# Running token tile 0 five jobs ahead in two blocks, with norm pieces transposed in that order and scaled by two engines

## The chip, the core and the metric

The kernel runs on one core of a Trainium2 chip. The core has a matmul engine (TensorE, PE in the profile), VectorE (DVE), ScalarE (ACT), GpSimd (POOL) and SyncE (SP), which run their own instruction queues in order, and DMA engines. The metric is the time of one execution in microseconds on the device.

## The reference

Two blocks follow each other on 256 tokens of width 2048, in float32. The first has two layers: a projection `x @ w_in`, two kinds of attention and a convolution, an output projection, and a layer norm. The second has an attention stage with a context, a gated merge of four branches, and a SwiGLU feed-forward network (FFN). What matters here are the places where a norm over the whole width stands between two matrix products:

```python
    y = jnp.concatenate([ya, yb, yc], axis=-1) @ w_out
    return layer_norm(ALPHA * x + y, ln_g, ln_b)      # then x @ w_in of the next layer
...
        x = x + g1 * merge_branches(h, branches, w_gate[i], w_branch, w_o[i])
        x = x + g2 * swiglu(modulate(rms_norm(x, norm2_w[i]), sh2, sc2),
                            w_ffn_gate[i], w_ffn_up[i], w_ffn_down[i])
```

A token's norm needs all 2048 columns of the product before it, and the product after it needs the normed row, transposed.

## The kernel before

**Products.** All large products run through `Kernel.run`. A block is one product of all 256 tokens (two token tiles t of 128) with 512 output columns. It is cut into jobs; a job brings 256 rows of the weights (512 KB). To keep float32 accuracy with fast matmuls, both factors are split into a high part (rounded, written by ScalarE) and a low part (what is left, written by VectorE), and each product is three matmuls: high x high, high x low weight, low x high weight. A unit is one 128-row half of a job with one tile, three matmuls; a step is four units, 12 matmuls, normally one job: halves kk = 0, 1, and within each the tiles 0 and 1. A block of 8 jobs has 96 matmuls.

**Steps.** Each step issues in this order: ScalarE's high parts of the weights that come up (`high`, L343; up to four jobs ahead, six buffers), one advance of each running background task (`step_tasks`), VectorE's low parts of the same weights (`low`, L351) with the load of a job four further on, perhaps a piece of another reduction on VectorE (`wmod_step`), and then its matmuls. The queues of the engines hold the instructions in just this order. A block may name `pre_t`, which makes the background task run on, at that place in the queues, until enough pieces are issued (`need`).

**Tail.** The last block ahead of a norm (of `w_out`, of `w_o`) has `tail` = 5: its last five jobs run with tile 0 first (10 units) and then with tile 1 (10 units), so that tile 0 is finished two and a half steps before tile 1. The sums of a finished tile are taken out of PSUM by `ev_out` or `ev_o` (VectorE, with statistics; a root on GpSimd), and at tile 0's end the norm's task is added.

**Pieces.** The task (`split_t`) works on eight pieces: column group g (512 columns) and tile t, in the order TILES = (0,0), (1,0), (0,1), (1,1), (2,0), (2,1), (3,0), (3,1). For each piece: a row-wise norm (`norm` L701 or `scaled` L792, on ScalarE; group 0 of the layer norm on VectorE), four 128 x 128 transposes on TensorE into one PSUM tile, four scalings by columns' scale and bias out of it on VectorE (tile `f`), the high part on ScalarE (L284) and the low part on VectorE. One round of the loop issues the low part of piece n-3, the scalings of piece n-1, norms up to two pieces ahead, the transposes of piece n and the high part of piece n-2. The task's first advance issues two norms; the second only yields.

**Boundaries.** The first block of layer 2 (columns 6656 on) and the FFN's first gate block have `pre_t`. READY = [3, 4, 6, 8] says how many pieces must be issued before a job of column group 0, 1, 2, 3 may run, so both tiles of group 0 before the first matmul. The task `lam` (two loads, a few VectorE instructions, an Exp) is started with the first block of a layer. The same `split_t` with scale and bias is used for the context (`context`) and for the norm between layer 2 and the second block (`layer_end` with l = 1, then `rms_t`); their blocks have no head.

Of the kernel before, what the change touches and what calls it, by code (L numbers as in the profile page):

```python
# [15 lines left out]
ALU = mybir.AluOpType  # L16
# [12 lines left out]
SPLIT = 1.15  # L29
LOOK = 4  # L30
ROWS = 13
TAIL, END = 5, 3

TILES = [(0, 0), (1, 0), (0, 1), (1, 1), (2, 0), (2, 1), (3, 0), (3, 1)]
READY = [3, 4, 6, 8]

WMOD_STEPS = {0: (22, 146), 1: (160, 274), 3: (290, 380), 4: (380, 470), 2: (470, 552), 5: (552, 612)}

# [74 lines left out]
class Block:  # L113


    def __init__(self, w, src, evac=None, pairs=None, pre=None, start=None, evac_t=None, pre_t=None, tail=0):
        self.w = w
        self.src = src
        self.evac = evac
        self.evac_t = evac_t  # L120
        self.pre_t = pre_t
        self.tail = tail
        self.pairs = list(range(w.shape[0])) if pairs is None else pairs
        self.pre = pre
        self.start = start
        self.ps = None


class Kernel:
# [99 lines left out]
        nc.gpsimd.tensor_tensor(r[:, 0:n], r[:, 0:n], self.half[:, 0:n], op=ALU.pow)  # L229
        return r  # L230

    def split_t(self, items, ahead=0):


        nc = self.nc
        n = 0
        xs = deque(it[0]() for it in items[:ahead])
        got = ahead
        yield n
        if ahead:  # L240
            yield n
        if items[0][3] is None:
            for src, hi, lo, _, _ in items:
                x = src()
                p = self.aux()
                for j in range(4):
                    nc.tensor.transpose(p[:, j * 128:(j + 1) * 128], x[:, j * 128:(j + 1) * 128], self.ident)
                yield n
                p3 = p.rearrange("p (j t) -> p j t", j=4)
                nc.scalar.activation(hi, p3, AF.Copy)  # L250
                yield n
                nc.vector.tensor_tensor(lo, p3, hi, op=ALU.subtract)
                n += 1
            yield n
            return
        ps, fs = {}, {}
        nt = nf = nh = nl = 0
        while nl < len(items):
            t, f, h = nt, nf, nh
            if nl < h:  # L260
                nc.vector.tensor_tensor(items[nl][2], fs.pop(nl), items[nl][1], op=ALU.subtract)
                nl += 1
            if nf < t:
                _, _, _, sc, bi = items[nf]
                p3 = ps.pop(nf).rearrange("p (j t) -> p j t", j=4)
                o = fs[nf] = self.h([128, 4, 128], name="f")
                for j in range(4):
                    nc.vector.tensor_scalar(o[:, j], p3[:, j], sc[:, j:j + 1], bi[:, j:j + 1],
                                            op0=ALU.mult, op1=ALU.add)
                nf += 1  # L270
            while got < min(nt + ahead + 1, len(items)):
                x = items[got][0]()
                if x is None:
                    break
                xs.append(x)
                got += 1
            if xs:
                x = xs.popleft()
                p = ps[nt] = self.aux()
                for j in range(4):  # L280
                    nc.tensor.transpose(p[:, j * 128:(j + 1) * 128], x[:, j * 128:(j + 1) * 128], self.ident)
                nt += 1
            if nh < f:
                nc.scalar.activation(items[nh][1], fs[nh], AF.Copy)  # L284
                nh += 1
            yield nl

    def pair(self, name):
        return (self.s([128, 4, 256], F32R, name=name + "h"), self.s([128, 4, 256], F32R, name=name + "l"))
# [16 lines left out]
    @staticmethod  # L306
    def order(jobs):


        units, i = [], 0  # L310
        while i < len(jobs):
            b, j = jobs[i]
            n = b.tail if b.tail and j == len(b.pairs) - b.tail else 0
            if n:
                units += [(i + m, kk, t) for t in range(2) for m in range(n) for kk in range(2)]
            else:
                units += [(i, kk, t) for kk in range(2) for t in range(2)]
            i += n or 1
        steps = [units[m:m + 4] for m in range(0, len(units), 4)]
        freed = {}  # L320
        for m, u in enumerate(steps):
            for n, _, _ in u:
                freed[n] = m
        return steps, freed
# [237 lines left out]
    def layer(self, l):  # L562
# [12 lines left out]
                self.at.pop(self.slot)[0]()  # L575

        def pre_t(k, t):
            self.need(self.xT_task, READY[k // 2])

        src = lambda k, t: self.src_of(xT)(k, t)  # L580

        def proj(c0, evac, first=False):
            self.block(w[c0 // 512], src, evac, pre_t=pre_t if first and l else None, start=start if first else None)

        def ev_sig(ps):
            st["sg"] = self.s([128, 2, 512], name="sg")
# [103 lines left out]
    def layer_end(self, l, r, stats):  # L690
# [35 lines left out]
        if l == 0 and len(rs) == 2:  # L726
            def gen():
                yield from self.wait(lambda: self.x_task, [self.xT_task])
                for g in range(4):
                    row(g)  # L730
                    yield
                    for t in range(2):
                        while self.room() < 0.6 and not self.x_task.forced:
                            yield
                        affine(g, t)
                        yield
                    keep(g)
            self.x_task = self.add(gen(), banks=0, rows=4)
        elif l == 0:
            self.xT = [self.pair("xT") for _ in range(4)]  # L740
            self.xT_task = self.add(self.split_t(
                [self.t_items(g, self.xT[g], norm, self.col("lng", g * 4, 4), self.col("lnb", g * 4, 4))[t]
                 for g, t in TILES], ahead=2), front=True)
        else:
            ss = self.m([128, 2, 4], name="ss")

            def gen():
                row(0)
                row(1)
                for g in range(6):  # L750
                    if g < 4:
                        for t in range(2):
                            norm(g, t)
                    if g >= 2:
                        for t in range(2):
                            self.square(r[g - 2][:, t], ss[:, t, g - 2:g - 1])
                        keep(g - 2)
                    yield
                    if 1 <= g < 5:
                        for t in range(2):  # L760
                            affine(g - 1, t)
                        yield
                        rows.pop(g - 1)
                        row(g + 1)
                yield from self.rms_t(r, ss, "sc1", "sh1")
            self.hT = [self.pair("hT") for _ in range(4)]
            self.h_dst = self.hT
            self.hT_task = self.add(gen(), front=True, rows=7)
# [8 lines left out]
        self.nc.vector.tensor_reduce(tot, ss[:, t], axis=AX.X, op=ALU.add)  # L777
        return self.rstd(tot, 1, 1.0 / D, RMS_EPS)

    def rms_t(self, r, ss, sc, sh, dst=None, rs=None):  # L780

        nc = self.nc
        dst = dst or self.h_dst
        if rs is None:
            rs = [self.rms(ss, t) for t in range(2)]
            yield

        def scaled(g, t):
            if len(rs) <= t:
                return None  # L790
            f = self.h([128, 512], name="xr")
            nc.scalar.activation(f, r[g][:, t], AF.Copy, scale=rs[t][:, 0:1])  # L792
            return f
        items = [self.t_items(g, dst[g], scaled, self.modc[sc][:, g * 4:g * 4 + 4], self.modc[sh][:, g * 4:g * 4 + 4])
                 for g in range(4)]
        yield from self.split_t([items[g][t] for g, t in TILES], ahead=2)

    def lam(self, l, lam_init, st):
        nc, a = self.nc, self.a
# [191 lines left out]
    def second(self):  # L991
# [14 lines left out]

        def h_pre(k):
            self.need_mod(0, 1)
            self.need(self.hT_task, READY[k // 2])

        hsrc = lambda k, t: self.src_of(hT)(k, t)
        csrc = lambda k, t: self.src_of(hc)(k, t)
# [155 lines left out]
        def ev_o(n):  # L1168
            def ev(t, ps):
# [8 lines left out]
                if n == 3 and t == 0:  # L1178
                    self.x_in = acc["xs"]
                    self.h_dst = self.h2T = [self.pair("h2T") for _ in range(4)]  # L1180
                    self.h2_task = self.add(self.rms_t(r, acc["ss"], "sc2", "sh2", rs=acc["rs"]), front=True, rows=7)
            return ev

        for n in range(4):
# [3 lines left out]
        f2 = lambda k, t: self.src_of(self.h2T)(k, t)  # L1188

        def h2_pre(k, t):  # L1190
            self.need(self.h2_task, READY[k // 2])

        aT = {}

# [27 lines left out]

        for part, js in ((0, range(0, 4)), (1, range(4, 8)), (2, range(8, 11))):
            for j in js:
                self.block(a["w_fg"][j], f2, ev_silu, pre_t=h2_pre if j == 0 else None)
                self.block(a["w_fu"][j], f2, ev_up(j))
            for n in range(4):
                self.block(a["w_fd"][n], lambda k, t: self.src_of(aT)(k, t), evac_t=ev_down(part, n),
                           pairs=[2 * j + i for j in js for i in range(2)],
                           pre=lambda k: self.need(st[f"f{k // 2}"]), start=load_x(n, xr),  # L1230
                           tail=END if (part, n) == (2, 3) else 0)
# [301 lines left out]
```

## Time and profile before

| | us |
|---|---|
| median of three runs | 2640.46 (2638.27 to 2641.5) |
| the profiled execution, its time | 2642.78 |
| the profiled execution, its span in the trace | 2640.9 |
| TensorE (matmuls) busy | 2611.5 |
| VectorE busy | 1802.6 |
| ScalarE busy | 1257.7 |
| GpSimd busy | 132.0 |

The shares are averages over the whole span. A matmul's duration in the rows (0.39 us for 512 columns) overlaps with the next; matmuls follow each other at 0.227 us. The granted clock stands in the views of stretches as a share of 2.4 GHz.

### The profile page before, as it was taken

The numbers are of one execution on the slowest core, as the hardware profiler recorded it, in microseconds if no ns is written. First come the engines' busy times: TensorE is split into PE (matmuls) and PEld (weight loads), VectorE is DVE, ScalarE is ACT, GpSimd is POOL, SyncE is SP. The second block draws the span as 40 slices with busy tenths as digits, with TensorE's granted clock in tenths as the row PEclk, the third lists the DMA queues.
The fourth block names the chain that finished last, engine by engine and source line by source line (L and its number), as shares of the span: only waits on it lengthen the run. The fifth ranks groups of instructions, "written<-read, shape, count | busy, mean of one in ns | idle before, by whom it ended". The sixth has DMA issues, their size and how long they took to land.

```text
span 2640.9 us, 32555 instructions
## 1 busy us (share of the span) xinstructions
PE 2611.5 (99%) x11902; PEld 2155.8 (82%) x11902; DVE 1802.6 (68%) x2516; ACT 1257.7 (48%) x1603; POOL 132.0 (5%) x193
## 2 busy tenths in 40 slices
PE   9999999999999999999999999999999999999999
PEld 7888888778888878887888888888788888888887
DVE  5898777799977788655766677777655554555444
ACT  6444753545466555444454444444544434443442
POOL 0000010000001020100200000000100000001000
PEclk9999999899999999999999999999999999999999
DMA  8776676676666788775776787888655576657664
GB/s 303 244 225 213 212 238 232 194 256 223 216 217 218 266 280 280 249 244 177 240 233 242 236 294 258 291 289 312 222 187 194 187 243 201 193 189 240 226 195 152
DMA packets 171233, 614.69 MB, mean 233 GB/s; under 512 B 19849, under 2 KB 20673, under 8 KB 171073
## 3 DMA queue, kind: packets, MB, share of 16 engines
q1 hardware_dynamic: 158400, 572.59, 64.9%
q0 software_dynamic: 11232, 37.24, 4.4%
q10 hardware_dynamic: 1440, 2.79, 0.3%
q8 instruction: 93, 1.52, 0.2%
q14 instruction: 68, 0.55, 0.1%
HBM read 599.92 MB, written 12.62 MB: 232 GB/s over the span
## 4 chain that ended last, share of the span: by engine, by line
PE 94%; DVE 2%; DMA 2%; issue 1%; POOL 0%; ACT 0%; SPq 0%; DVEq 0%; ACTq 0%; POOLq 0%
PE mm L75 88%; PE aux L75 6%; DMA raw<-in_w_in 1%; DVE lo L351 1%; DMA raw<-in_w_out 1%; DMA row<-in_ln_b 1%; DVE f L75 0%; DVE res L75 0%; ACT hi L343 0%; POOL rstd L229 0%; DVE wmjunk L75 0%; POOL rstd L228 0%; DVE xTl L75 0%; DVE gate L75 0%; DVE h2Tl L75 0%
## 5 line engine op out<-in xcount | busy, mean ns | idle before, releaser
L351 DVE TENSOR_TENSOR lo<-raw,hi 128x1024 fp32r<-128x1024 f32 (+1 forms) x893 | 1077.9, 1220 | 641.8 <-ACT hi L343 640.9
L343 ACT ACTIVATE hi<-raw 128x1024 fp32r<-128x1024 f32 (+1 forms) x893 | 936.6, 1059 | 1028.0 <-PE mm L75 832.1
L75 PE MATMUL mm<-hi,xTh 128*128 128x512 f32 x960 | 385.3, 401 | 6.0 <-ACT hi L343 5.9
L75 PE MATMUL mm<-hi,xTl 128*128 128x512 f32 x960 | 377.2, 393 | 1.1 <-DVE xTl L75 1.1
L75 PE MATMUL mm<-lo,xTh 128*128 128x512 f32 x960 | 376.2, 392 | 0.0
L75 PE MATMUL mm<-hi,hTh 128*128 128x512 f32 x864 | 343.6, 398 | 0.0
L75 PE MATMUL mm<-hi,hTl 128*128 128x512 f32 x864 | 336.9, 390 | 0.0
L75 PE MATMUL mm<-lo,hTh 128*128 128x512 f32 x864 | 336.4, 389 | 0.0
L75 DVE CUSTOM_DVE_ANT_0 wmjunk<-wm,c 128x1024 bf16<-128x1024 f32 x256 | 312.4, 1220 | 4.7 <-DMA wm<-in_w_mod 2.4
L75 PE MATMUL mm<-hi,h2Th 128*128 128x512 f32 x704 | 276.0, 392 | 0.1
L75 PE MATMUL mm<-hi,h2Tl 128*128 128x512 f32 x704 | 274.5, 390 | 1.1 <-DVE h2Tl L75 1.1
L75 PE MATMUL mm<-lo,h2Th 128*128 128x512 f32 x704 | 274.3, 390 | 0.0
L75 PEld LDWEIGHTS mm<-hi,xTh 128*128 128x128 f32 x960 | 181.9, 189 | 43.4 <-ACT hi L343 5.9
L75 PEld LDWEIGHTS mm<-hi,xTl 128*128 128x128 f32 x960 | 181.4, 189 | 41.3 <-DVE xTl L75 2.2
L75 PEld LDWEIGHTS mm<-lo,xTh 128*128 128x128 f32 x960 | 181.9, 189 | 35.9 <-DVE lo L351 0.4
L75 PEld LDWEIGHTS mm<-hi,hTl 128*128 128x128 f32 x864 | 162.2, 188 | 34.4
L75 PEld LDWEIGHTS mm<-lo,hTh 128*128 128x128 f32 x864 | 162.4, 188 | 32.8 <-issue 0.2
L75 PEld LDWEIGHTS mm<-hi,hTh 128*128 128x128 f32 x864 | 162.3, 188 | 32.4 <-issue 0.5
L75 PEld LDWEIGHTS mm<-hi,h2Tl 128*128 128x128 f32 x704 | 132.3, 188 | 29.1 <-DVE h2Tl L75 1.5
L75 PEld LDWEIGHTS mm<-hi,h2Th 128*128 128x128 f32 x704 | 132.4, 188 | 27.5 <-ACT h2Th L284 0.8
L75 PEld LDWEIGHTS mm<-lo,h2Th 128*128 128x128 f32 x704 | 132.4, 188 | 26.9
L75 PE MATMUL mm<-hi,yTh 128*128 128x512 f32 x384 | 150.9, 393 | 0.0
(274 smaller groups left out, 3061.0 us busy)
## 6 DMA issues: line engine op xcount, KB each, us to landing
raw<-in_w_in SPq DMA_DIRECT2D x360, 512.0 KB, 4.4
wm<-in_w_mod SPq DMA_DIRECT2D x192, 512.0 KB, 4.8
raw<-in_w_gate SPq DMA_DIRECT2D x128, 512.0 KB, 4.7
raw<-in_w_fg SPq DMA_DIRECT2D x88, 512.0 KB, 4.4
raw<-in_w_fu SPq DMA_DIRECT2D x88, 512.0 KB, 3.8
raw<-in_w_fd SPq DMA_DIRECT2D x88, 512.0 KB, 4.3
raw<-in_w_out SPq DMA_DIRECT2D x64, 512.0 KB, 4.6
raw<-in_w_o SPq DMA_DIRECT2D x32, 512.0 KB, 5.2
```

Source lines behind the costliest of these rows:

```text
L75: return f(*args, **kw)
L343: nc.scalar.activation(hi[:, k], t[:, k], AF.Copy)
L351: nc.nc.vector.tensor_tensor(lo[:, k], t[:, k], hi[:, k], op=ALU.subtract)
```

## The change

It adds a `head` to blocks: in the first block of layer 2 and in the FFN's first block the first five jobs run with tile 0 first (10 units) and then with tile 1. The pieces of the two norms come in the order AHEAD, which has tile 0 of groups 0, 1 and 2 first, and `ready` counts pieces for a job and a tile. With `quick` the task does without its second, empty advance and runs its first two rounds in one. Of the four scalings of a piece, columns 1 and 3 go to ScalarE; this is in `split_t` and holds for all four users of scale and bias.

```diff
-TAIL, END = 5, 3
+TAIL, END, HEAD = 5, 3, 5
...
 TILES = [(0, 0), (1, 0), (0, 1), (1, 1), (2, 0), (2, 1), (3, 0), (3, 1)]
-READY = [3, 4, 6, 8]
+AHEAD = [(0, 0), (1, 0), (2, 0), (0, 1), (1, 1), (2, 1), (3, 0), (3, 1)]
+
+def ready(tiles, k, t):
+    return tiles.index((k // 2, t)) + 1
...
-    def split_t(self, items, ahead=0):
+    def split_t(self, items, ahead=0, quick=False):
...
-        if ahead:
+        if ahead and not quick:
             yield n
...
                 for j in range(4):
-                    nc.vector.tensor_scalar(o[:, j], p3[:, j], sc[:, j:j + 1], bi[:, j:j + 1],
-                                            op0=ALU.mult, op1=ALU.add)
+                    if j % 2:
+                        nc.scalar.activation(o[:, j], p3[:, j], AF.Identity, scale=sc[:, j:j + 1], bias=bi[:, j:j + 1])
+                    else:
+                        nc.vector.tensor_scalar(o[:, j], p3[:, j], sc[:, j:j + 1], bi[:, j:j + 1],
+                                                op0=ALU.mult, op1=ALU.add)
...
-            yield nl
+            if quick:
+                quick = False
+            else:
+                yield nl
...
-            n = b.tail if b.tail and j == len(b.pairs) - b.tail else 0
+            n = b.tail if b.tail and j == len(b.pairs) - b.tail else b.head if j == 0 else 0
...
-            self.need(self.xT_task, READY[k // 2])
+            self.need(self.xT_task, ready(AHEAD, k, t))
...
-            self.block(w[c0 // 512], src, evac, pre_t=pre_t if first and l else None, start=start if first else None)
+            self.block(w[c0 // 512], src, evac, pre_t=pre_t if first and l else None, start=start if first else None,
+                       head=HEAD if first and l else 0)
...
-                 for g, t in TILES], ahead=2), front=True)
+                 for g, t in AHEAD], ahead=2, quick=True), front=True)
...
-        yield from self.split_t([items[g][t] for g, t in TILES], ahead=2)
+        yield from self.split_t([items[g][t] for g, t in tiles], ahead=2, quick=quick)
...
-            self.need(self.hT_task, READY[k // 2])
+            self.need(self.hT_task, ready(TILES, k, 1))
...
-                    self.h2_task = self.add(self.rms_t(r, acc["ss"], "sc2", "sh2", rs=acc["rs"]), front=True, rows=7)
+                    self.h2_task = self.add(self.rms_t(r, acc["ss"], "sc2", "sh2", rs=acc["rs"], tiles=AHEAD, quick=True), front=True, rows=7)
...
-            self.need(self.h2_task, READY[k // 2])
+            self.need(self.h2_task, ready(AHEAD, k, t))
...
-                self.block(a["w_fg"][j], f2, ev_silu, pre_t=h2_pre if j == 0 else None)
+                self.block(a["w_fg"][j], f2, ev_silu, pre_t=h2_pre if j == 0 else None, head=0 if j else HEAD)
```

## Rows read from the trace of the kernel before

**Rows 1.** The page: busy us (share of span), instructions.
```profile
PE 2611.5 (99%) x11902; PEld 2155.8 (82%) x11902; DVE 1802.6 (68%) x2516; ACT 1257.7 (48%) x1603; POOL 132.0 (5%) x193
```

**Rows 2.** Stretches: us, PE busy (matmuls) [first: all engines], granted clock, DMA share, GB/s.
```profile
440.00:460.00 20.00, 20.00 (x90) 16.54 (x90) 12.55 (x19) 6.78 (x7) 0.00 (x0) 1.00 0.69 237
...
472.00:473.00 1.00, 0.15 (x1) 0.68 0.94 385
...
486.00:487.00 1.00, 1.00 (x6) 0.99 0.97 242
...
1905.00:1906.00 1.00, 0.92 (x3) 0.52 0.25 90
```

**Rows 3.** Timeline, TensorE, first boundary: start, us, engine, line, instruction, idle before.
```profile
469.07 1.04 PE L75 MATMUL aux<-ident,res 128*128 128x128 f32 x8
472.85 1.94 PE L75 MATMUL aux<-ident,res 128*128 128x128 f32 x8 [2.74 <-DVE res L75]
...
477.30 0.78 PE L75 MATMUL mm<-hi,xTh 128*128 128x512 f32 x1
...
480.79 0.79 PE L75 MATMUL mm<-hi,xTl 128*128 128x512 f32 x1 [0.59 <-DVE xTl L75]
```

**Rows 4.** Timeline, TensorE, second boundary.
```profile
1895.08 1.03 PE L75 MATMUL aux<-ident,xr 128*128 128x128 f32 x8
1900.51 2.82 PE L75 MATMUL aux<-ident,xr 128*128 128x128 f32 x12 [4.40 <-ACT xr L792]
...
1904.22 0.78 PE L75 MATMUL mm<-hi,h2Th 128*128 128x512 f32 x1
...
1907.74 0.50 PE L75 MATMUL mm<-hi,h2Tl 128*128 128x512 f32 x1 [1.08 <-DVE h2Tl L75]
```

**Rows 5.** Timeline, VectorE, first boundary.
```profile
472.16 0.54 DVE L75 TENSOR_SCALAR res<-res,mv,rstd 128x512 f32<-128x512 f32 x1
...
473.75 2.64 DVE L75 TENSOR_SCALAR f<-aux,cols 128x128 f32<-128x128 f32 x8
476.31 0.68 DVE L75 TENSOR_TENSOR xTl<-f,xTh 128x512 fp32r<-128x512 f32 x1
```

**Rows 6.** Timeline, ScalarE, second boundary.
```profile
1891.82 1.34 ACT L792 ACTIVATE xr<-res,rstd 128x512 f32<-128x512 f32 x2 [0.21 <-POOL rstd L229]
1893.06 1.99 ACT L343 ACTIVATE hi<-raw 128x1024 fp32r<-128x1024 f32 x2
...
1905.25 0.63 ACT L284 ACTIVATE h2Th<-f 128x512 fp32r<-128x512 f32 x1 [0.63 <-DVE f L75]
```

**Rows 7.** Timelines, VectorE and ScalarE: one head's query and key.
```profile
1351.36 0.48 DVE L75 TENSOR_SCALAR qk<-aux,qns 128x256 f32<-128x256 f32 x1
1351.88 0.48 ACT L1276 ACTIVATE qk<-aux,cols 128x256 f32<-128x256 f32 x1 [2.07 <-DVE qk L75]
```

**Rows 8.** ScalarE's groups by line and shape: count, busy us, mean ns, idle before.
```profile
L916 ACT ACTIVATE sc<-aux 128x128 f32<-128x128 f32 x16 | 4.1, 263 | 0.0
L982 ACT ACTIVATE csilu<-aux,cols 128x256 f32<-128x256 f32 x8 | 4.1, 562 | 0.1
...
L969 ACT ACTIVATE z<-aux,nm,rstd 128x512 f32<-128x512 f32 x4 | 3.1, 782 | 7.8 <-DVE nm L75 7.8
```

**Rows 9.** Timeline, ScalarE, first boundary.
```profile
466.06 2.95 ACT L343 ACTIVATE hi<-raw 128x1024 fp32r<-128x1024 f32 x3
```

**Rows 10.** The lambda load's tile (dl): issue to landing.
```profile
DMA to landing us min/median/max: 2.8/3.8/4.7
```

**Rows 11.** Timeline, VectorE, second boundary.
```profile
1896.41 0.68 DVE L75 TENSOR_TENSOR tmp<-mm,gb 128x512 f32<-128x512 f32 x1
```

**Rows 12.** Timelines of TensorE, ScalarE and VectorE at the norm after layer 2.
```profile
1002.28 0.60 PE L75 MATMUL aux<-ident,xr 128*128 128x128 f32 x4
...
997.54 0.71 ACT L792 ACTIVATE xr<-res,rstd 128x512 f32<-128x512 f32 x1
...
998.94 1.36 DVE L75 TENSOR_SCALAR f<-aux,sc,sh 128x128 f32<-128x128 f32 x4
```

More of the change, by code (lines that the diff above doesn't have):

```diff
@@ L113, with __init__ @@
 class Block:
-    def __init__(self, w, src, evac=None, pairs=None, pre=None, start=None, evac_t=None, pre_t=None, tail=0):
+    def __init__(self, w, src, evac=None, pairs=None, pre=None, start=None, evac_t=None, pre_t=None, tail=0,
+                 head=0):
         self.w = w
@@ L122, in __init__ @@
         self.tail = tail
+        self.head = head
         self.pairs = list(range(w.shape[0])) if pairs is None else pairs
@@ L778, in rms, with rms_t @@
         return self.rstd(tot, 1, 1.0 / D, RMS_EPS)
-    def rms_t(self, r, ss, sc, sh, dst=None, rs=None):
+    def rms_t(self, r, ss, sc, sh, dst=None, rs=None, tiles=TILES, quick=False):
         nc = self.nc
```

## Prediction

> **What bounds the kernel now.** I read the page's busy shares first: TensorE is busy 99% of the span [rows 1], so an edit pays or costs only where TensorE stands or runs slowly. The next view, stretches with the granted clock, shows where: a full stretch holds 90 matmuls in 20 us, 0.22 us each (0.227 between neighbouring starts), and the clock falls from 1.00 to 0.50, which is its lower level of 1.2 GHz, twice: from about 472.3 to 486 us, and until about 1906 us [rows 2]. These are the two block boundaries that the change rewrites. I then read TensorE's timeline there. First boundary: the last block's matmuls end at 469.1; eight transposes follow, then 2.74 us of nothing, slow transposes (eight take 1.94 us instead of 1.04), the first matmul at 477.30, and a stall of 0.59 us before the one at 480.79 [rows 3]. Second: eight transposes at 1895.08, 4.40 us of nothing, slow transposes, first matmul 1904.22, a stall of 1.08 us before the sixth at 1907.74 [rows 4]. The block that begins there has 96 matmuls (0.227 us) and 32 transposes (0.09 us, from eight in 1.04 less the tail of the last): 24.7 us of work. Counted on from the sixth matmul (480.79 and 1907.74; 0.43 us each while the clock is low), the first block of layer 2 ends near 504.9 and took 35.8 us from 469.1; that of the FFN ends near 1929.4 and took 34.3 from 1895.1. So about 11.1 and 9.6 us are lost there, and that is the most the change can win: 20 us, 0.8%.
>
> What ends last in these stretches is VectorE. At the first boundary its queue holds the norm of tile 1 (472.16) before the first scaling; eight scalings run from 473.75, and the first low part comes at 476.31 [rows 5]. One piece costs VectorE a low part of 0.6 and four scalings of 0.32 spacing, 1.9 us in all.
>
> **The change, part by part.** *Order and head.* Tile 0 of five jobs needs only pieces (0,0), (1,0), (2,0), so the first matmul waits for one finished piece instead of three. No matmul, transpose or DMA is added or removed. The weights' copies are due earlier: the split of the fifth head job is read in the third step of the head instead of the fifth. ScalarE writes its high half at about 470 and VectorE its low half before 477.5, both ahead of that step; no cost. The reserve of six split buffers holds, because job 13's copies come before the head's first release.
>
> *Two more rounds before the boundary (quick).* Transposes of the first two pieces, and scaling of the first, move in front of the last step of the previous block. TensorE pays 8 x 0.09 = 0.72 us there, which the idle time hid before. At the first boundary the norms are ready by 466.2, when that step starts. At the second, the step begins at 1892.36, but ScalarE ends the two scaled rows only at 1893.16 [rows 6]: the 0.36 us of transposes wait 0.3 and 0.25 more, 1.3 us in all.
>
> *Scaling shared by two engines.* This decides. Columns 0 and 2 go to VectorE, 1 and 3 to ScalarE, out of one transposed tile in PSUM. The trace of before has one such pair: the query part of a head is scaled by VectorE, the key part by ScalarE, out of one PSUM tile into disjoint halves of another. ScalarE starts 0.04 us after VectorE ends, having waited 2.07 us for it [rows 7]. Nothing in the data asks for it. It is not the destination tile either: the first FFN matmul reads one half of a tile at 1904.22 while the other half is written later, at 1905.25 [rows 4, 6]. So two engines reading one PSUM tile are put in order. I take it both ways: VectorE, ScalarE, VectorE, ScalarE, each waiting for the one before.
>
> The row shows one direction only. The Trainium skill, PSUM — Partial Sum Buffer, section "PSUM bank collisions raise a hardware error", states that two engines on one bank collide, reads against reads included, and that the compiler's scheduler makes any two such instructions dependent. By that rule the second direction holds too and the sharing buys no parallel work; without it the first rival below would be the forecast.
>
> The price of a piece: VectorE's scaling 0.40. ScalarE's is not in the trace in this shape. With scale and bias columns 512 elements take 0.78 and 256 take 0.56, so 128 take about 0.46; a 128-element square without columns takes 0.26 [rows 8]. I take 0.46, since its form is that of the first two, and keep 0.26 as the low end. The chain is 0.40 + 0.46 + 0.40 + 0.46 and three handoffs of 0.04: 1.84 us, against 1.36 for four on VectorE (eight take 2.64 [rows 5]). Worse, both engines run their queues in order, so what stands behind a scaling waits for the other engine's queue. From one high half to the next the loop is now: low part 0.65, the chain 1.84, a norm 0.7 on ScalarE while any are left, high half 0.63, one handoff more: 3.8 us with a norm, 3.1 without. TensorE uses up a piece in 24.7/8 = 3.1. Before, the loop was 1.9.
>
> *First boundary.* In the last step ScalarE's queue is: two weight copies (466.06, 1.0 each), the norm of (2,0), then its first scaling at about 468.7 [rows 9]. VectorE does column 0 at 467.0 and stands until 469.15. Behind it stand two weights' low parts and all of tile 1's evacuation, which so starts 2.3 us later, at 471.8; the norm's inputs come at 474.4 (the norm itself ran at 472.16). Then piece 1's chain, the norm of (0,1) at 476.2, for which TensorE's fourth transpose waits, and the high half of piece 0 at 477.5. First matmul 477.6, against 477.30, with 16 transposes still to come instead of 8. High halves follow at 481.3, 485.1 and 488.8 (3.8 each), then near 492 and 495; TensorE wants the fourth (tile 1, group 0) at 487.9. On VectorE the lambda task stands before that piece's low part: its load lands 2.8 to 4.7 us after its issue [rows 10], which is at about 485 here, so up to 1.6 us more. The last two pieces come behind two weight copies and the table load of the Exp: their low parts end at about 501 and 502.5 to 504. After the last 19 matmuls remain, 4.3 us: end 506.8 to 508.4 against 504.9, a loss of 1.9 to 3.5. With 0.26 on ScalarE, two times 0.2 less for seven pieces, 2.8 less. I take +2.3, range -1 to +3.5. [...]
>
> *Second boundary.* VectorE stands at column 2 of piece 0 until 1896.1, behind ScalarE's copies (1893.06, 1.99) and a third row [rows 6]; two low parts follow, and tile 1's evacuation starts at 1898.7 instead of 1896.41 [rows 11]. Square, sum and root as before, then a weight copy and piece 1's chain ahead of the row that the fourth transpose needs: 1903.9. High half of piece 0 at 1905.2, first matmul 1905.3 (was 1904.22). High halves at 1908.8, 1912.4, 1916.1, then 3 us apart; the last two low parts at 1927.6 and 1929.4, behind weights. The end is 1929.45 + 19 x 0.227 = 1933.8 against 1929.4, +4.3; with the low ScalarE price +1.5. I take +3.7.
>
> *The two stages that keep their order.* The context and the norm between layer 2 and the second block use the same helper, so their scalings are shared too. In the latter, rows on ScalarE are asked for two pieces ahead: row 5 at 997.54 for a transpose at 1002.28, 4 us in hand. With ScalarE's queue behind the chain of piece 2, which VectorE reached at 998.94 [rows 12], row 5 ends near 1003, row 6 near 1007.3, row 7 near 1011: stalls of 0.9, 1.0 and 0.4 us. I take +1.8, bounds 0 and 3.5. In the context stage the same sum leaves 1.3 us in hand; no cost, but 3 us if that is gone.
>
> Sum: 2.3 + 3.7 + 1.8 = +7.8 us. The profiled execution took 2642.78 us, 1.9 more than its span and 2.3 above the median of 2640.46; a profile of after would be near 2650.6, the median near 2648.3.
>
> **The rivals.** (a) The reads are not ordered both ways; ScalarE only follows VectorE's first column. Then a piece costs VectorE 0.7 instead of 1.3, and it stands nowhere. Tile 1's evacuation starts at 470.1, first matmul 474.6 with xTl 0.5 later; TensorE runs unbroken from 475.9, and if the clock rises between the 1.8 us after the first matmul of [rows 4] and the 5.2 us after the stall of [rows 3], the first boundary gains about 4.0 (2.9 to 4.6). The second starts at 1902.6 and gains about 1.7. Sum -5.7: 2634.8. This ends on the other side, and the point that decides is whether VectorE's column 2 waits for ScalarE's column 1. For it: only one direction is seen. Against: [rows 7] show a wait with no data behind it, and a reason for one direction is one for the other.
>
> (b) The order holds, but the head's matmuls cover the late pieces (cheap ScalarE, its queue emptier than I have it, no stall at the norm stage): +0 and +1.5 at the boundaries, 2642. For it: TensorE's 3.1 per piece is just the loop without a norm.
>
> (c) The coupled queues starve the weights as well, in the context and norm stages: 4 us more, 2652. Against: copies run four jobs ahead, some 11 us.
>
> **How the numbers follow.** Forecast 0.47, (a) 0.14, (b) 0.29, (c) 0.10. The forecast's own range is 2644.5 to 2651; with (b) and part of (a) the range becomes 2636 to 2651.5. A measurement can tell 0.2%, 5.3 us, from no change. Faster is (a) with a first boundary at least as good as forecast, 0.12. Slower is (c) and most of the forecast, 0.55. The rest, 0.33, is the same.
>
> **What would show it.** Right: VectorE's scaling groups wait for ScalarE's and the reverse; no scalings of a piece overlap; first matmuls at about 477.6 and 1905.3; TensorE waits for high or low parts inside the head. Wrong: two engines' scalings of one piece at one time, or first matmuls near 474.6 and 1902.6. Steps to check besides: 8 transposes ahead of the last step, tile 1's evacuation 2.3 us later, transposes at the norm stage waiting for rows.

## The result, and the profile of the changed kernel

The changed kernel took 2661.29 us (median of 4 runs, 2657.43 to 2661.8) beside 2640.85 us (4 runs, 2638.27 to 2641.5) for the kernel before: a ratio of 1.0071, 95% interval 1.0058 to 1.0083. The forecast was 2648.3 with a range up to 2651.5. The direction holds, and so does the step that was to decide it, the order between the two engines. The size doesn't: one term was too small, one had the wrong mechanism, and one of the largest costs was not in the sum. The profiled execution took 2661.58 us with a span of 2659.8, 18.9 us more than the span before.

The page, first part (busy us, share of the span, instructions), answers [rows 1]:

```profile
PE 2616.4 (98%) x11902; PEld 2156.0 (81%) x11902; DVE 1786.2 (67%) x2452; ACT 1280.4 (48%) x1667; POOL 130.7 (5%) x193
```

TensorE's instructions are the same in number. It is idle for 2659.8 - 2616.4 = 43.4 us, against 29.4 before: 14.0 us more. The other 4.9 us are the same matmuls run longer, at the lower clock.

The view of waits of the changed kernel (engine, line, what it waited for: us in total, times, longest):

```profile
ACT f L280 <- DVE f L83: 37.5, 46, 4.0
...
DVE f L83 <- ACT f L280: 24.4, 32, 2.7
...
PE aux L83 <- ACT xr L810: 11.4, 3, 6.6
...
PE aux L83 <- DVE res L83: 5.8, 1, 5.8
...
PE aux L83 <- DVE sg L83: 5.4, 1, 5.4
```

The first two lines are the forecast's decisive step: each engine's scalings wait for the other's, in both directions. The last three are where TensorE pays. The wait for `res` and the longest one for `xr` belong to the boundaries; a second one for `xr`, of 4.6 us, stands at the norm after layer 2. The third line, a wait for the gate evacuation `sg`, stands in no part of the prediction (before it came to 1.8 us in all).

First boundary, TensorE (start us, us, engine, line, instruction, idle before and what ended it), answers [rows 3]:

```profile
466.16 1.03 PE L83 MATMUL aux<-ident,res 128*128 128x128 f32 x8
...
469.79 0.60 PE L83 MATMUL aux<-ident,res 128*128 128x128 f32 x4
476.23 1.08 PE L83 MATMUL aux<-ident,res 128*128 128x128 f32 x4 [5.84 <-DVE res L83]
...
488.50 0.50 PE L83 MATMUL mm<-hi,xTh 128*128 128x512 f32 x1 [0.66 <-ACT xTh L298]
...
499.71 0.50 PE L83 MATMUL mm<-hi,xTh 128*128 128x512 f32 x1 [0.55 <-ACT xTh L298]
...
501.85 0.54 PE L83 MATMUL mm<-hi,xTl 128*128 128x512 f32 x1 [1.40 <-DVE xTl L83]
...
503.59 0.80 PE L83 MATMUL mm<-hi,xTl 128*128 128x512 f32 x1 [0.34 <-DVE xTl L83]
504.18 0.63 PE L83 MATMUL mm<-hi,xTh 128*128 128x512 f32 x1
504.61 0.63 PE L83 MATMUL mm<-lo,xTh 128*128 128x512 f32 x1
```

The same stretch on VectorE, answers [rows 5]:

```profile
466.80 0.41 DVE L83 TENSOR_SCALAR f<-aux,cols 128x128 f32<-128x128 f32 x1
468.95 0.41 DVE L83 TENSOR_SCALAR f<-aux,cols 128x128 f32<-128x128 f32 x1 [1.74 <-ACT f L280]
469.28 2.35 DVE L368 TENSOR_TENSOR lo<-raw,hi 128x1024 fp32r<-128x1024 f32 x2
471.55 0.68 DVE L83 SCALAR_TENSOR_TENSOR res<-res,mm 128x512 f32<-128x512 f32 x1
```

and on ScalarE, answers [rows 9]:

```profile
468.48 0.43 ACT L280 ACTIVATE f<-aux,cols 128x128 f32<-128x128 f32 x1
...
476.73 0.62 ACT L298 ACTIVATE xTh<-f 128x512 fp32r<-128x512 f32 x1
...
480.43 0.62 ACT L298 ACTIVATE xTh<-f 128x512 fp32r<-128x512 f32 x1
...
484.13 0.62 ACT L298 ACTIVATE xTh<-f 128x512 fp32r<-128x512 f32 x1
```

VectorE scales column 0 at 466.80, stands until ScalarE, behind its weight copies, has scaled column 1 (468.48), and only then reaches the two low parts and tile 1's evacuation (471.55). The high halves come 3.70 us apart. The transposes of the fourth piece (tile 1's first) wait 5.84 us on TensorE, and the last pieces come late.

Second boundary, TensorE, answers [rows 4]:

```profile
1911.33 0.60 PE L83 MATMUL aux<-ident,xr 128*128 128x128 f32 x4
1918.57 1.12 PE L83 MATMUL aux<-ident,xr 128*128 128x128 f32 x4 [6.65 <-ACT xr L810]
1919.70 0.79 PE L83 MATMUL mm<-hi,h2Th 128*128 128x512 f32 x1
...
1930.53 0.50 PE L83 MATMUL mm<-hi,h2Th 128*128 128x512 f32 x1 [1.23 <-ACT h2Th L298]
```

The stall that was not foreseen comes 30 us after the end of layer 2's first block. VectorE of the changed kernel there:

```profile
535.21 0.69 DVE L83 TENSOR_TENSOR res<-res,row 128x512 f32<-128x512 f32 x1 [3.76 <-DMA row<-in_ln_g]
536.55 0.69 DVE L83 TENSOR_TENSOR res<-res,row 128x512 f32<-128x512 f32 x1 [0.64 <-DMA row<-in_ln_b]
...
538.29 1.28 DVE L83 TENSOR_TENSOR sg<-mm,sg 128x512 f32<-128x512 f32 x2
```

TensorE, same stretch:

```profile
539.03 1.50 PE L83 MATMUL aux<-ident,sg 128*128 128x128 f32 x4 [5.44 <-DVE sg L83]
```

and VectorE of the kernel before at the same work:

```profile
530.42 1.28 DVE L75 TENSOR_TENSOR sg<-mm,sg 128x512 f32<-128x512 f32 x2
...
538.68 1.42 DVE L75 TENSOR_TENSOR res<-res,row 128x512 f32<-128x512 f32 x2 [5.84 <-DMA row<-in_ln_g]
```

A background task finishes layer 1's residual once all pieces are made: it multiplies by a row of scales and adds a row of shifts that it loads group by group (`row`, on GpSimd's queue; landing 3.9 to 8.6 us after the issue, median 7.3). Before, VectorE met the longest wait for a row (5.84 us) behind the evacuation `sg`. In the changed kernel one such wait (3.76) falls just in front of it, and TensorE waits for `sg`.

### The profile page after: what moved, and what is told of

Read it like the earlier page. It is cut to its first block, busy times and chain, and to the rows that moved or that the text cites. A ratio compares the mean times of both kernels' runs of the same rounds, so it can differ in the third digit from the quotient of the medians.

```text
span 2659.8 us, 32544 instructions
## 1 busy us (share of the span) xinstructions
PE 2616.4 (98%) x11902; PEld 2156.0 (81%) x11902; DVE 1786.2 (67%) x2452; ACT 1280.4 (48%) x1667; POOL 130.7 (5%) x193
## 4 chain that ended last, share of the span: by engine, by line
PE 90%; DVE 4%; ACT 2%; DMA 2%; issue 1%; POOL 0%; SPq 0%; DVEq 0%; ACTq 0%; POOLq 0%
PE mm L83 84%; PE aux L83 6%; DVE lo L368 1%; DMA raw<-in_w_in 1%; DVE f L83 1%; DMA raw<-in_w_out 1%; ACT hi L360 1%; ACT f L280 1%; DVE wmjunk L83 1%; DMA row<-in_ln_b 1%; DVE res L83 0%; ACT xr L810 0%; POOL rstd L239 0%; DVE xTl L83 0%; DVE hcTl L83 0%
```

## Where the time went, by stretch

To compare kernels I divide each profiled execution at five marks: the start of the last matmul ahead of the first boundary (L1), ScalarE's first evacuation of layer 2's first block (sg), of the block called `bq` (bq), the start of the last matmul ahead of the FFN (L2), and the first evacuation of the FFN's first block (fg). In kernels with the two earlier rounds (`quick`: the changed one, e1, e3, e4, e5, e7, e9, e10) eight transposes stand ahead of L1 and of L2, 0.7 us each time, and ahead of L2 they wait as much again: from the evacuation of the block `vc` to L2 it is about 855.0 us instead of 853.6 (856.6 in the changed kernel's profile, by a fall of the clock that is told of below). So against a kernel without quick the first column is to be read 0.7 longer, and the fourth 1.4. Times in us:

| kernel | median | L1 to sg | sg to bq | bq to L2 | L2 to fg | fg to end |
|---|---|---|---|---|---|---|
| before | 2640.85 | 35.6 | 47.0 | 1343.4 | 34.1 | 711.9 |
| changed | 2661.29 | 38.9 | 52.2 | 1350.4 | 36.7 | 712.0 |
| e1_vector_only | 2643.84 | 31.4 | 53.6 | 1344.5 | 31.5 | 711.9 |
| e2_share_alone | 2669.65 | 40.9 | 58.2 | 1347.9 | 41.3 | 712.0 |
| e3_two_banks | 2645.03 | 30.1 | 52.7 | 1345.4 | 31.1 | 712.0 |
| e4_rows_early | 2652.63 | 39.4 | 44.5 | 1348.7 | 36.7 | 712.0 |
| e5_vector_rows_early | 2636.11 | 30.9 | 44.5 | 1345.8 | 30.1 | 711.9 |
| e6_before_rows_early | 2641.03 | 33.2 | 46.3 | 1345.3 | 34.2 | 711.9 |
| e7_two_banks_rows | 2636.69 | 31.1 | 44.5 | 1344.4 | 31.1 | 712.0 |
| e8_vector_rows_not_quick | 2636.90 | 32.9 | 44.6 | 1342.0 | 33.6 | 711.9 |
| e9_halves_vector_first | 2639.54 | 33.4 | 45.2 | 1346.6 | 31.7 | 711.9 |
| e10_halves_scalar_first | 2644.68 | 35.9 | 45.0 | 1343.7 | 34.2 | 711.9 |
| e11_order_alone | 2643.24 | 34.6 | 44.5 | 1344.8 | 35.5 | 711.9 |

The experiments ran on three chips (e1 to e4, e5 to e8, e9 to e11). The kernel before had medians of 2640.41, 2640.82 and 2641.57 us on them, so up to 1.2 us of a difference between medians of two groups can be the chip's.

Each row is one execution, and e6 shows what that is worth. It differs from before at the first boundary only in two row loads that GpSimd issues earlier, and TensorE's long wait there is the same 2.74 us, yet the stretch is 2.4 us shorter. The granted clock of before (stretch: us, PE busy with matmuls, granted clock, DMA share, GB/s):

```profile
475.00:480.00 5.00, 4.50 (x13) 0.50 0.48 145
480.00:485.00 5.00, 4.41 (x13) 0.50 0.14 40
```

and of e6:

```profile
475.00:480.00 5.00, 3.80 (x13) 0.67 0.80 244
480.00:485.00 5.00, 4.68 (x22) 1.00 0.15 42
```

The clock of before is low until 486 us, that of e6 until about 478. So a difference of under 2.5 us in one boundary's column tells nothing by itself; verdicts below rest on the medians, or on columns that differ by more.

## The experiments

**Sharing undone.** All four scalings of a piece go to VectorE again; head, order and quick stay.

```diff
-                    if j % 2:
-                        nc.scalar.activation(o[:, j], p3[:, j], AF.Identity, ...)
-                    else:
-                        nc.vector.tensor_scalar(o[:, j], p3[:, j], ...)
+                    nc.vector.tensor_scalar(o[:, j], p3[:, j], ...)
```

> The changed kernel with all four scalings of a piece back on VectorE; head, order and quick stay. Theory 1 (the two engines take turns on one PSUM tile, and their queues with them): the loop per piece falls from 3.7 to 1.9 us, tile 1's evacuation at the first boundary starts near 470.5 instead of 471.6, first matmul near 475.5 instead of 477.4, no stall inside the head; the first boundary ends 2.5 to 4 us before that of the kernel before, the second about 1.7 before; the norm after layer 2 loses nothing. About 2636 us, and up to 5 more if the stall of the gated product after the first boundary stays. Theory 2 (the head with its two extra rounds ahead of the boundary is what costs): near 2655 us, as the changed kernel.

Measured 2643.84 us (1.0007, 0.9998 to 1.0016). Sharing costs 2661.3 - 2643.8 = 17.4 us of the 20. With the 0.7 and 1.4 added both boundaries are shorter than before, by 3.5 and 1.2 us (1.1 and 1.3 against e6's profile), but the stall at `sg` stays, with 6.1 us on TensorE. So that stall doesn't need the sharing. I had expected 2636 and up to 5 more if the stall stayed; it is 2.8 above that.

**Sharing alone.** The kernel before with nothing but the shared scaling.

```diff
+                    if j % 2:
+                        nc.scalar.activation(o[:, j], p3[:, j], AF.Identity, ...)
+                    else:
                         nc.vector.tensor_scalar(o[:, j], p3[:, j], ...)
```

> The kernel before with the shared scaling alone; its order of pieces, no head, no quick. Theory 1: the chain paces all eight pieces at both boundaries, with three pieces due before the first matmul, and the norm after layer 2 waits for its rows: 5 to 7 us at each boundary and 3.7 at the norm, 2652 to 2658 us. Theory 2: within 3 us of the kernel before, 2640.

Measured 2669.65 us (1.0103, 1.0089 to 1.0117), 8 us worse than the whole change. Its view of waits:

```profile
PE aux L75 <- ACT xr L795: 14.4, 5, 5.2
...
PE aux L75 <- DVE sg L75: 10.2, 1, 10.2
```

Head and order hide a part of what sharing costs: without them TensorE needs the pieces of both tiles at once and waits for five rows instead of three, and for `sg` 10.2 us. The stall at `sg` doesn't need the head either: here the sharing alone moves the boundary, and it comes. My expectation was 12 us too low mainly because, like the prediction, it priced no stall behind the boundaries (sg to bq is 11.2 us longer than before).

**Two transposed tiles.** Columns 0 and 2 are transposed into one PSUM tile, 1 and 3 into another, so the engines never read the same one. They still write into the same tile `f`.

```diff
-                p = ps[nt] = self.aux()
+                pq = ps[nt] = [self.aux(), self.aux()]
                 for j in range(4):
-                    nc.tensor.transpose(p[:, j * 128:(j + 1) * 128], ...)
+                    nc.tensor.transpose(pq[j % 2][:, j // 2 * 128:j // 2 * 128 + 128], ...)
```

> The changed kernel, but the transposes of columns 0 and 2 go to one PSUM tile and those of 1 and 3 to another, so the two engines share the scalings without sharing a PSUM tile. Theory 1 says that the order between the engines vanishes: the waits of VectorE's scalings for ScalarE's and of ScalarE's for VectorE's go from 24 and 38 us to under 3, the loop per piece to about 2 us, and both boundaries end before those of the kernel before: the 5.7 us that the first rival was priced at, about 2635 us, up to 5 more if the stall of the gated product stays. If sharing costs by ScalarE's load alone (theory 3), the waits stay small but the time stays above 2650 us.

Measured 2645.03 us (1.0013, 1.0004 to 1.0022). The two lines of waits between the engines' scalings are gone. VectorE of this kernel:

```profile
477.39 0.72 DVE L83 TENSOR_SCALAR f<-aux,cols 128x128 f32<-128x128 f32 x2
```

and ScalarE:

```profile
477.53 0.79 ACT L281 ACTIVATE f<-aux,cols 128x128 f32<-128x128 f32 x2
```

They run at the same time. So the order was due to the shared source tile, and the destination has no part in it. This is the first rival made real. It priced the boundaries at -4.0 and -1.7; measured, with the 0.7 and 1.4 added, 30.8 against 35.6 and 32.5 against 34.1: -4.8 and -1.6 (-2.4 and -1.7 against e6's profile). The time is 5 us above what I expected, because the stall at `sg` costs more than the 5 us that I allowed for it: e7 shows 8.3.

By the rule of the Trainium skill that the prediction cites (PSUM — Partial Sum Buffer, section "PSUM bank collisions raise a hardware error"), two engines on one bank are made dependent; e3 agrees, 0 waits between the scalings on two tiles against 78 on one. No run here shows what the reads would do if nothing put them in order.

**Row loads one group ahead.** The changed kernel, the rows of a group asked for before the group in front of it is worked on.

```diff
+                row(0)
+                yield
                 for g in range(4):
-                    row(g)
-                    yield
+                    row(g + 1)
```

> The changed kernel, but the background task that finishes layer 1's residual requests each pair of scale and shift rows one group ahead. Theory: VectorE stood for a row (2.95 and 3.76 us) ahead of the gate's evacuation in its queue, and TensorE's convolution transposes stood 5.4 us for that, after which the clock fell; with the row there in time 5 to 6 us come back: about 2655 us, and no wait of TensorE for the gated product over 1.5 us. If the loads' traffic delays the weights instead (rival), the stall moves to the weights and the time stays at 2661 us.

Measured 2652.63 us (1.0042, 1.0029 to 1.0055): 8.7 us less than the changed kernel, where I had expected 5 to 6; it is the largest single part after the sharing. VectorE comes to the evacuation without a wait for a row in front of it:

```profile
529.21 1.41 DVE L83 TENSOR_TENSOR res<-res,row 128x512 f32<-128x512 f32 x2
...
531.67 1.28 DVE L83 TENSOR_TENSOR sg<-mm,sg 128x512 f32<-128x512 f32 x2
```

TensorE is busy throughout, and sg to bq is 44.5 us instead of 52.2. That the stall comes from the rows is thereby shown. The column of bq to L2 is 1.7 shorter besides, of which 0.75 is idle time of TensorE; a fall of the clock that only the changed kernel's profile has is told of below.

**The same with all scalings on VectorE.** e1 and the edit of e4 together.

> All scalings on VectorE (as in e1_vector_only) and, besides, the row loads of the residual task asked for one group ahead (as in e4_rows_early). If the stall at the gate's evacuation is a cost of its own, independent of the sharing, the landmark of the second block loses 5 to 6 us as it did in e4: 2643.8 - 5.5 = about 2638.3, and TensorE shows no wait of several us for VectorE's sigmoid evacuation. If the stall was only the backlog of a late x_task, it comes back elsewhere and the time stays at 2642 to 2644.

Measured 2636.11 us (0.9982, 0.9973 to 0.9991), 7.7 less than e1 and faster than the kernel before. Against e4 it prices the sharing by itself, with no stall at `sg` in either: 2652.6 - 2636.1 = 16.5 us. By the columns 8.5 of them lie at the first boundary, 6.6 at the second and 2.9 between bq and L2.

**The kernel before with early rows.** The edit of e4 alone.

> The kernel before with the row loads asked for one group ahead, and nothing else. In the kernel before TensorE waits 1.8 us in all for the sigmoid evacuation and the rows' long wait (5.84 us) stands behind that evacuation. If the stall is a product of the moved boundary, there is little to win here: 2638.5 to 2640.5. If row loads cost the kernel before as much as the changed one, 2635.

Measured 2641.03 us (1.0000, 0.9991 to 1.0009). Before, the wait stood behind the evacuation, and taking it away gains nothing. The row loads became a cost only because the boundary moved under them.

**Two tiles and early rows.** e3 and the edit of e4.

> Two transposed tiles for each piece (as in e3_two_banks) and the row loads one group ahead. e3 began its second block at -4.2 us and lost 5.7 us up to bq; without that stall bq should stand near -4 and the FFN's first block near -5: 2645.0 - 5.5 = about 2639.5 by the medians, or 2635 by the landmarks (the profile of e3 was 2.6 us below its median). Faster than the kernel before if the first boundary's gain survives.

Measured 2636.69 us (0.9982, 0.9973 to 0.9991), the same as e5 with VectorE alone (2636.11). Sharing that really runs in parallel gains nothing that can be measured here. It fits that VectorE's scalings are no longer what TensorE waits for once order and head are changed: TensorE's long wait at the first boundary is for tile 1's norm, 4.66 us in e5 and 3.74 in e7.

**Without the two earlier rounds.** e5, `quick` left out at both calls.

> As e5_vector_rows_early but without the two earlier rounds of transposes and scaling (quick), so only head and order are left. If quick brings its scalings ahead of the previous block's evacuation at a gain, the first boundary ends some 1 to 2 us later than in e5 (landmark sg -1 instead of -2.5) and the time is 1 to 3 us more. If quick delays tile 1's evacuation by as much as it gains, no difference.

Measured 2636.90 us (0.9985, 0.9976 to 0.9994): 0.8 us more than e5, within the intervals. Whether quick gains is not settled. By the columns it wins 2.0 - 0.7 = 1.3 us at the first boundary and 3.5 - 1.4 = 2.1 at the second; both are within what one execution can show. Its own cost ahead of the second boundary, the 1.4 us, was forecast at 1.3.

**One handoff, VectorE first.** e4, but VectorE scales columns 0 and 1, then ScalarE 2 and 3, out of one tile.

```diff
-                    if j % 2:
+                    if j >= 2:
```

> The changed kernel with row loads one group ahead (as e4_rows_early, 2652.6), but each piece is shared in two halves: VectorE scales columns 0 and 1, then ScalarE columns 2 and 3, still out of one transposed tile. One handoff instead of three, and VectorE never stands inside a piece. With all scalings on VectorE and the same row loads the kernel took 2636.1, so sharing costs 16.5 us there. Theory A, the loss comes from VectorE standing behind ScalarE's queue with the evacuations and low parts behind it: most of the 16.5 goes, 2637 to 2643. Theory B, the loss comes from the chain's length and from ScalarE's queue being in it at all: the chain is 1.7 us instead of 1.84, 2648 to 2653.

Measured 2639.54 us (0.9987, 0.9978 to 0.9996): 13.1 of the 16.5 us are gone, with the same work on each engine and the same tile. VectorE at the first boundary (`lo` between the two lines):

```profile
465.89 0.73 DVE L83 TENSOR_SCALAR f<-aux,cols 128x128 f32<-128x128 f32 x2
...
469.07 0.69 DVE L83 SCALAR_TENSOR_TENSOR res<-res,mm 128x512 f32<-128x512 f32 x1 [0.19 <-PE mm L83]
```

VectorE does its half at once and begins tile 1's evacuation as soon as TensorE is done, 0.4 us after L1 (468.64), against 2.0 in the changed kernel (471.55 and 469.56). The time is as theory A has it. What the 3.4 us are that remain against e5 was not traced.

**One handoff, ScalarE first.** e4 with the halves the other way round.

```diff
-                    if j % 2:
+                    if j < 2:
```

> As e9_halves_vector_first with the halves the other way round: ScalarE scales columns 0 and 1 first, then VectorE 2 and 3. Again one handoff, but now VectorE stands once in each piece until ScalarE's queue has come to it. Theory A: VectorE stands as long as in the alternating kernel, 2649 to 2656. Theory B: the same as e9. If the two kernels differ by under 3 us, the direction of the wait doesn't matter.

Measured 2644.68 us (1.0009, 1.0000 to 1.0017). VectorE:

```profile
469.39 0.73 DVE L83 TENSOR_SCALAR f<-aux,cols 128x128 f32<-128x128 f32 x2 [2.59 <-ACT f L280]
...
472.30 0.68 DVE L83 SCALAR_TENSOR_TENSOR res<-res,mm 128x512 f32<-128x512 f32 x1
```

Tile 1's evacuation is even later than in the changed kernel, 2.6 us after L1 (469.65), yet the kernel is 8 us better than e4. Theory A in its simple form, that VectorE's first standing is the whole loss, put it at 2649 or more and misses. The direction of the one wait is worth 5.1 us (e10 less e9); the alternating form, with two handoffs more, costs another 8.0 (e4 less e10).

**Order alone.** e8 with `HEAD` 0: the pieces in the new order, the first block's jobs in the old one.

> As e8_vector_rows_not_quick (2636.9) but without the head: the pieces come in the new order, tile 0's three groups first, and the first block's matmuls go in the old order, both tiles of a job together. The second job's tile 1 then needs the fourth piece, where the old order gave it the third. If the head is what gains, this loses all of it and a little more: 2639 to 2643. If the new order of pieces gains by itself (tile 0's pieces fill the wait for tile 1's statistics), 2636 to 2638.

Measured 2643.24 us (1.0004, 0.9995 to 1.0012): 6.3 more than with the head (e8), and 2.2 more than the old order with early rows (e6). The new order by itself gains nothing; with it, the head gains 6.3. The head in the old order was not run.

## Why the prediction was right and wrong

**Right: two engines reading one PSUM tile are put in order both ways.** Inferred from one pair in one direction [rows 7], where the destination is an operand of TensorE and not a second PSUM tile; shown by the two lines of waits, and its cause by e3. The estimate for ScalarE's scaling, 0.46 us, from two larger shapes [rows 8], is what the rows show (0.43 to 0.46).

**Right: the first boundary's course up to its tail.** Tile 1's evacuation was put at 471.8 and came at 471.55; the norm's inputs at 474.4 (474.21); the first matmul at 477.6 (477.40); the loop at 3.8 us with a norm and 3.1 without (3.70 and 3.0); the ends of the last two low parts at about 501 and 502.5 to 504 (501.80 and 503.53).

**Wrong in size: the first boundary's term.** It was +2.3, range -1 to +3.5, and is +4.0 (38.9 + 0.7 - 35.6). The step that failed is the price of the last 19 matmuls: 0.227 us each, 4.3 in all. From 503.59 on they took 5.4 us: behind the stalls at 499.71 and 501.85 the clock fell a second time, to its lower level of 1.2 GHz (a mean of 0.83 from 499.56 to 509.56), and from 502.19 to 505.46 matmuls start about 0.43 us apart. I had matmuls at that pace only at a boundary's start. The other 0.6 us are the last low part: +2.3 means an end near 502.9, and it came at 503.53.

At the boundary's start the clock hid a part of the loss. It was low from 474.9 to 481.7 us, against 472.4 to 486.0 before, so 4.8 us more of idle time (8.88 against 4.05 between L1 and sg) make the column only 3.3 longer. Against e6's column the term would be 6.4: its size hangs on the execution of before that it is held against.

**Right: the second boundary.** Forecast +3.7; the column gives 36.7 - 34.1 = +2.6, and the way to L2 1.4 more: +4.0, the same within what one execution shows. Its parts shifted: the first matmul came 8.6 us after L2 (1919.70 and 1911.09), where the forecast's 1905.3 meant 9.2; stalls inside the block, such as the 1.23 us at 1930.53, give that back.

**Wrong in mechanism: the norm stage.** Forecast +1.8 by three stalls for rows 5 to 7. Those came to 0.2 us. What grew is the wait for the stage's first row, from 3.0 to 4.6 us. Changed kernel:

```profile
996.82 1.33 ACT L810 ACTIVATE xr<-res,rstd 128x512 f32<-128x512 f32 x2 [5.01 <-POOL rstd L239]
```

```profile
997.59 1.12 PE L83 MATMUL aux<-ident,xr 128*128 128x128 f32 x4 [4.62 <-ACT xr L810]
```

and before:

```profile
986.25 0.66 PE L75 MATMUL aux<-ident,xr 128*128 128x128 f32 x4 [2.98 <-ACT xr L792]
```

The clock fell at this wait, to a mean of 0.83 over 10 us, which before it did not. The wait ends ahead of the stage's first scaling, which needs these transposes, so the chain that I priced can't be what lengthens it. Over the runs it is 5.2, 4.6 and 3.9 us in the three kernels with alternating sharing (e2, changed, e4) and 0.8 to 3.3 in the others; in e6, with VectorE scaling alone, it is 3.3 and the clock falls as well. So sharing may have a part in it by what stands earlier in the queues, but no run shows how; that cause stays open. The context stage, at 0, has no idle time of TensorE, as forecast.

**Missing: the stall at the gate.** The term was put at nothing, without a reason. It is +5.2 us in the changed kernel (3.7 of idle time, the rest slower matmuls behind it), and 7.7 by e4's column. Taking the row waits away gives back 7.7 to 8.7 us by the medians (e1 to e5, e3 to e7, changed to e4). The prediction followed each queue past the scalings up to the end of the two blocks and stopped there. It named no work that was waiting for the pieces to be done: the residual's task starts when the last piece is made, and its loads' 7.3 us to land put a wait of VectorE in front of an evacuation on which TensorE depends. "What is late next" should have been asked for every task that waits for the moved one.

**Missing: one more fall of the clock.** Near 1245 us before and 1260 us in the changed kernel TensorE has the same idle time of 2.3 us. Before, the clock stayed at 1.00 there; in the changed kernel's profile:

```profile
1255.00:1260.00 5.00, 2.67 (x16) 0.99 0.00 0
1260.00:1265.00 5.00, 5.00 (x21) 0.67 0.27 84
```

That is 1.7 us of matmuls (5 us at a third less than full speed). None of the other twelve profiles shows it, e4's with the same sharing neither, so nothing here ties it to the change.

The account of the 18.9 us: first boundary 4.0, gate 5.2, norm stage 3.3 (1.6 idle and 1.7 of clock), second boundary 4.0, the fall near 1260 1.7; together 18.2, and 0.7 that I can't place. By the medians the runs divide the 20.4 us in another way: order, head and quick gain 4.7 when the rows come early (e5 against before, where early rows alone gain nothing: e6), the sharing costs 16.5 (e4 against e5) and the late rows 8.7 (changed against e4). Even with all three terms of the forecast at their upper bounds (3.5, 4.3 and 3.5) the sum gives 2651.8, so within its own bounds the forecast could not reach the result.

**The rivals.** The first one's prices agree with e3 as far as one execution can show (against before's profile, and less at the first boundary against e6's), but its total of 2634.8 would not have come either: with the gate's stall e3 is at 2645.0, and 2636.7 without (e7). The second, that the chain is covered, is refuted by the 16.5 us between e4 and e5. The third, starved weights, took no part: TensorE's wait for `hi` is 6.2 us in the changed kernel, 5.9 before and 5.8 in e5. The rival that was missing is a stage beyond the boundaries, as above.

## What to carry to other kernels

Two engines that read one PSUM tile in turns ran one after the other here, and each dragged the other's whole queue along: give each engine a tile of its own, or hand over once, away from the engine whose queue holds the critical work, and not back (16.5 us alternating, 8.6 and 3.4 with one handoff, 0.6 on two tiles, each against VectorE alone). Before sharing work, look whether the engine is still what ends last once the order is changed; here VectorE's scalings cost nothing that could be won back once head and order were in (e5 and e7 alike), and the best kernels (e5, e7) gain 0.18%, one without sharing and one with it. When a stage is moved in time, follow also the tasks that start when it ends, with their loads.

## What the runs showed of the hardware that was not expected

The granted clock is not settled by the program alone. Over 27 executions of the kernel before (those beside e9 to e11) its mean was 0.995 in the three longest, 2645.7 to 2647.6 us, and 0.998 in the shortest, 2638.8. In the profiles it was low until 486 us before and until about 478 in e6, behind the same wait of 2.74 us, and at a later stall of 2.3 us that both kernels have it fell in the changed kernel and not before. Row loads on GpSimd's queue (512 columns, broadcast to all partitions) need 7.3 us to land by the median; asked for at the moment of need they cost nothing behind the critical evacuation (e6) and 7.7 us of sg to bq in front of it (e4).
